# The low part of every second down-projection weight unit, made by a negated cast and an adding DMA

## The chip, the cores and the metric

The kernel runs on one NeuronCore of one Trainium2 chip. The core has a matmul engine (TensorE, in the profile PE for the matmuls and PEld for the weight loads that overlap them), three engines for elementwise work (VectorE or DVE, ScalarE or ACT, GpSimd or POOL) and SyncE (SP), which here only issues DMAs. Each engine works through its own queue in order and waits for others by semaphores. Sixteen DMA engines move data between HBM and SBUF, the on-chip memory of 128 partitions; matmuls write to PSUM. DMAs can be issued from the queues of SP, ACT and POOL.

The metric is the device time of the program in microseconds (us), as the median of several runs. The profile is one further execution, recorded instruction by instruction.

## The reference

The reference is a two-layer decoder trunk on 256 tokens of width 2048, in float32. Layer 0 mixes with gated linear attention, layer 1 with a causal attention that has forget gates; both attend to 256 memory tokens as well. What bears on this change is the channel mixer, which each layer ends with:

```python
def conv_ffn(h, w_up, conv_w, conv_b, w_down):
    u = causal_dwconv(h @ w_up, conv_w, conv_b)
    a, val = split_cols(u, [FFN_HIDDEN, FFN_HIDDEN])
    return (jax.nn.silu(a) * val) @ w_down
```

`FFN_HIDDEN` is 5632, so the down projection multiplies a 256 x 5632 activation by a 5632 x 2048 weight and adds the product to the residual stream, `x = x + conv_ffn(h, ...)`, once for each of the two layers.

## The kernel before

**Two parts for each number.** TensorE multiplies numbers in a shortened float32 (type `fp32r` in the profile). To keep accuracy, weights and activations are each held as a high part, which is the value rounded to that type, and a low part, the value minus its high part. A product is then three matmuls: high by high, high activation by low weight, low activation by high weight. Activations sit in SBUF with both parts (`bufA` and `bufB`, tiles A and B in the profile). Weights come from HBM once, in full float32, and are split on the way.

**Weight units.** The host lays all weights out as one array `wp`, cut into units of mostly 128 x 1024 float32 (512 KB). For the down projections a unit holds two blocks of 128 hidden channels by 512 output columns. The function `load_unit` (lines 185 to 200) takes a unit in: SP issues the DMA into a tile `raw` (line 196, four buffers), and ACT casts `raw` to the high part `whi` (line 199, three buffers). `split_unit` (line 202) calls it and then has DVE subtract, `wlo = raw - whi` (line 208, three buffers). Both `whi` and `wlo` go through their three buffers in turn, so the cast of a unit can start only when the matmuls of the unit three places before it have ended.

**The two kinds of projection.** `proj_fm` (used for the up projections; matmuls at lines 233, 234 and 236) has channels on the output's partitions. `proj_tm` (line 246; matmuls at lines 270, 271 and 272) has tokens there; the down projections go through it. For one unit it issues 12 matmuls: two halves of the tokens, two channel blocks, three products. Line 270 is high by high, line 271 uses the low part of the weight, line 272 the high part again with the low part of the activation. The weights are the moving operand, so each of the 12 streams 512 columns.

**Stages.** `ffn` (line 780) cuts the 5632 hidden channels into three parts of 16, 16 and 12 blocks of 128 (`PARTS`). For each part it runs the up projections of that part, which leave the activations in A or B, and then four down projections of 512 output columns each, added to the residual stream by DVE at line 774. So a down stage has 4 x 8, 4 x 8 or 4 x 6 units, a layer has 88 and the kernel 176. In the last projection of layer 1 a pool named `spare` holds units 3 to 5, and the second half of the tokens runs four units behind the first.

**What sets the order.** The program is written as one sequence; a scheduler orders each engine's queue by priorities and by its own estimates of time. Loading and splitting of a unit stand in a block of raised priority (`AHEAD`, 300 places ahead), so casts and subtractions are put as early as their buffers allow. In the order that results, the matmuls of a down unit begin with two of line 270, one for each half of the tokens, before the first of line 271.

Of the kernel before, what the change touches and what calls it, by code (L numbers as in the profile page):

```python
# [13 lines left out]
F32R = mybir.dt.float32r  # L14
I32 = mybir.dt.int32
AF = mybir.ActivationFunctionType
ALU = mybir.AluOpType
PSUM = bass.MemoryType.PSUM

P = 128  # L20
# [17 lines left out]
NUNIT = 1024  # L38
AHEAD = 300
# [99 lines left out]
def _trunk(ctx: ExitStack, tc: tile.TileContext, xt, xtok, memt, wp, wgu, gns, gfin, cnv, par, msk, out):  # L139
    nc = tc.nc  # L140
    where, _ = _layout()
    V, S, TE = nc.vector, nc.scalar, nc.tensor

    const = ctx.enter_context(tc.tile_pool(name="const", bufs=1))
    wpool = ctx.enter_context(tc.tile_pool(name="wpool", bufs=4))
# [39 lines left out]
    def load_unit(unit, pieces=1, before=None, pool=wpool, whole=False):  # L185
        off, kcs, n = unit
        w = len(kcs) * n
        raw = wpool.tile([P, NUNIT], F32, name="raw", tag="raw", bufs=4)
        hi = pool.tile([P, NUNIT], F32R, name="whi", tag="whi", bufs=3)
        src = wp[off : off + P * w].rearrange("(p n) -> p n", p=P)  # L190
        for i in range(pieces):
            if before is not None:
                before(i)
            s = slice(i * w // pieces, (i + 1) * w // pieces)
            if not whole:
                loads.append(nc.sync.dma_start(raw[:, s], src[:, s]))
            elif i == 0:
                loads.append(nc.sync.dma_start(raw[:, :w], src))
            casts.append(S.activation(hi[:, s], raw[:, s], AF.Copy))  # L199
        return raw, hi, w  # L200

    def split_unit(unit, pieces=1, before=None, pool=wpool, whole=False):
        with tc.high_priority(offset=AHEAD):
            raw, hi, w = load_unit(unit, pieces, before, pool, whole)
            lo = pool.tile([P, NUNIT], F32R, name="wlo", tag="wlo", bufs=3)
            for i in range(pieces):
                s = slice(i * w // pieces, (i + 1) * w // pieces)
                V.tensor_tensor(lo[:, s], raw[:, s], hi[:, s].bitcast(F32), ALU.subtract)  # L208
        return hi, lo

    def proj_fm(key, src, evac, before=None):

        units = where[key]
        total = sum(len(u[1]) for u in units)
        acc = [pacc.tile([P, 512], F32, name="acc", tag="acc") for _ in range(2)]
        base = min(min(u[1]) for u in units)
        done = 0
        for n, unit in enumerate(units):
            if before is None:
                hi, lo = split_unit(unit)  # L220
            else:
                hi, lo = split_unit(unit, 2, lambda half: before(n, half), whole=n > 0)
            for j, kc in enumerate(unit[1]):
                for c in range(2):
                    product(acc[c], c, total - 1, done, src[kc - base], hi, lo, j)
                done += 1
        for c in range(2):
            evac(c, acc[c])
# [17 lines left out]
    def proj_tm(key, src, evac, spare=None):  # L246

        units = where[key]  # L250
        n = units[0][2]
        base = min(min(u[1]) for u in units)
        acc = [pacc.tile([P, 512], F32, name="acc", tag="acc") for _ in range(2)]
        ahead = 0 if spare is None else 4
        ready = {}
        for i in range(len(units) + ahead):
            for b, u in ((0, i), (1, i - ahead)):
                if not 0 <= u < len(units):
                    continue
                if b == 0:  # L260
                    ready[u] = split_unit(units[u], pool=wpool if spare is None or u < 3 else spare)
                hi, lo = ready[u]
                kcs = units[u][1]
                a = acc[b][:, :n]
                xs = slice(b * P, (b + 1) * P)
                for j, kc in enumerate(kcs):
                    s = slice(j * n, (j + 1) * n)
                    xk = src[kc - base]
                    last = u == len(units) - 1 and j == len(kcs) - 1
                    TE.matmul(a, xk[:, 0, xs], hi[:, s], start=u == 0 and j == 0, stop=False)  # L270
                    TE.matmul(a, xk[:, 0, xs], lo[:, s], start=False, stop=False)  # L271
                    TE.matmul(a, xk[:, 1, xs], hi[:, s], start=False, stop=last)  # L272
                if u == len(units) - 1:
                    evac(b, a)
# [138 lines left out]
    with tc.tile_pool(name="load", bufs=1) as lp:  # L413
# [55 lines left out]
        with tc.issue_after(loads[-1].ins):  # L469
            for i in range(KC):  # L470
                nc.sync.dma_start(xf[i], xt[i])
            nc.sync.dma_start(part, par)
            nc.sync.dma_start(mask[:, M_FOX:], msk[:, M_FOX:])
        proj_tm(("mv", 0), bufA, mv_out(0))
        for i in range(KC):
            split(bufB, i, xf[i], gain("mix0", i))
        for j in range(2):
            proj_fm(("mk", 1, j), bufA, mk_out(1, j))
            if j == 0:
# [3 lines left out]
                for f in range(4):  # L483
                    for b in range(2):
                        nx.add(f, b)
        proj_tm(("mv", 1), bufA, mv_out(1))


    def gla(nx):
        h, mix = bufB, bufA  # L490
        with tc.tile_pool(name="gla", bufs=1) as gp:
# [14 lines left out]
            def first_values(b, a):  # L506
                S.activation(v0[:, b, :], a[:, :DV], AF.Copy, scale=nx.col()[:, b : b + 1])
                take(b, a[:, DV:])
                if b:
                    S.activation(glr, turn(), AF.Copy)  # L510

            proj_tm(("gv", 0), h, first_values)

            def take_mq(j):
# [297 lines left out]
    def preparing(name, dst, also=None):  # L812
        n = StreamNorm()

        def then(f, b):
            n.add(f, b)
            if b == 0:
                return
            for i in range(4 * f, 4 * f + 4, 2):
                ps = work("s", 2)  # L820
                for j in range(2):
                    for c in range(2):
                        o = j * T + c * P
                        k = (i + j) % 4 * P
                        TE.transpose(ps[:, o : o + P], x[f][:, c, k : k + P], ident)  # L825
                for j in range(2):
                    split(dst, i + j, ps[:, j * T : (j + 1) * T], gain(name, i + j))
                if also is not None:
                    also(i, ps)

        return n, then

    gla(nx)
    n, then = preparing("ffn0", bufB)
# [14 lines left out]
    n, then = preparing("ffn1", bufA)  # L849
# [104 lines left out]
```

## Time and profile before

| what | value |
|---|---|
| median of the runs | 2302.16 us (2302.14 to 2302.43, 3 runs) |
| span of the profiled execution, first to last instruction | 2300.7 us |
| PE busy | 2286.8 us |
| PEld busy | 1977.8 us |
| DVE busy | 1614.6 us |
| ACT busy | 1252.9 us |
| POOL busy | 3.0 us |
| read from HBM | 425.87 MB |

The profiled execution's own time is taken as its span of 2300.7 us; the 1.5 us by which the median of the unprofiled runs stands above it lie before the first and behind the last instruction.

How to read the rows: the page begins with the busy time of each engine, then a strip of 40 equal time slices, then the DMA queues, the chain of work that ended last, the costliest groups of instructions and the DMA issues. A group's row names its line, engine and operation, `out<-in` with the program's tile names, the shape, how often it ran (`x`), its busy time, the mean duration of one in ns, and then the idle time of that engine directly before these instructions with what ended it. A view of waits lists who waited for whom. A timeline lists single instructions with their start in us from the beginning of the span, their duration, and in brackets the idle time before them. Matmuls are pipelined: each is listed with 0.39 us from its start to its modelled end, while the next starts 0.23 us after it, so a busy PE is not a count of work. "us to landing" is the time from the issue of a DMA until its data are known to have arrived.

### The profile page before, as it was taken

What the parts mean: (1) busy time and instruction counts of PE and PEld (TensorE: products, weight loads), DVE (VectorE), ACT (ScalarE), POOL (GpSimd) and SP (SyncE); (2) the same over time, 40 slices, a digit from 0 to 9 for tenths busy, and PEclk for the clock granted to TensorE, in tenths of its full rate; (3) what the DMA queues carried; (4) which work ended last, traced back from release to release, by engine and by line L of the source; (5) the groups of instructions that cost most, each with busy time, mean ns of one, the idle gap of its engine ahead of it and who ended that gap; (6) DMA issues with size and microseconds to landing.
All of it is one profiled execution on the core that took longest, in us unless ns stands there. A gap on an engine that the chain in (4) does not pass through costs nothing.

```text
span 2300.7 us, 33144 instructions
## 1 busy us (share of the span) xinstructions
PE 2286.8 (99%) x12392; PEld 1977.8 (86%) x12392; DVE 1614.6 (70%) x2639; ACT 1252.9 (54%) x1961; POOL 3.0 (0%) x19
## 2 busy tenths in 40 slices
PE   9999999999999999999999999999999999999998
PEld 7889888888888888888888998888888888888886
DVE  7568987577765777557767557657776577756775
ACT  7555565555553555445565555556554455534554
POOL 0000000000000000000000000000000000000000
PEclk9999999999999999999999999999999999999999
DMA  8644455555555555555555564555555555555554
GB/s 317 196 160 160 150 165 177 187 182 190 190 190 194 187 191 189 192 191 189 190 183 185 180 194 158 166 191 188 186 191 192 192 187 189 190 195 191 186 190 156
DMA packets 124745, 430.15 MB, mean 187 GB/s; under 512 B 14108, under 2 KB 18600, under 8 KB 124456
## 3 DMA queue, kind: packets, MB, share of 16 engines
q1 hardware_dynamic: 124152, 427.24, 55.7%
q8 instruction: 97, 1.59, 0.3%
q10 hardware_dynamic: 432, 0.79, 0.1%
q14 instruction: 64, 0.52, 0.1%
HBM read 425.87 MB, written 2.11 MB: 186 GB/s over the span
## 4 chain that ended last, share of the span: by engine, by line
PE 99%; DMA 0%; ACT 0%; DVE 0%; issue 0%; SPq 0%; DVEq 0%; ACTq 0%
PE acc L233 37%; PE acc L234 20%; PE acc L271 12%; PE acc L272 12%; PE acc L270 12%; PE acc L236 2%; PE ps_s L825 0%; PE ps_s L614 0%; PE ps_t L388 0%; PE ps_s L395 0%; PE ps_o L406 0%; DMA mt<-memt 0%; PE ps_s L739 0%; PE ps_o L633 0%; PE ps_o L755 0%; PE ps_s L533 0%
## 5 line engine op out<-in xcount | busy, mean ns | idle before, releaser
L208 DVE TENSOR_TENSOR wlo<-raw,whi 128x1024 fp32r<-128x1024 f32 (+4 forms) x812 | 972.7, 1199 | 547.3 <-ACT whi L199 533.3
L199 ACT ACTIVATE whi<-raw 128x1024 fp32r<-128x1024 f32 (+4 forms) x812 | 843.5, 1040 | 775.7 <-PE acc L272 370.6
L233 PE MATMUL acc<-B,whi 128*128 128x512 f32 x1980 | 684.1, 396 | 0.0
L233 PE MATMUL acc<-A,whi 128*128 128x512 f32 x1680 | 579.1, 396 | 1.9 <-DVE A L300 1.5
L234 PE MATMUL acc<-B,wlo 128*128 128x256 f32 x2112 | 551.2, 281 | 0.0
L234 PE MATMUL acc<-A,wlo 128*128 128x256 f32 x1792 | 463.9, 281 | 0.7 <-DVE wlo L208 0.7
L233 PEld LDWEIGHTS acc<-B,whi 128*128 128x128 f32 x1980 | 360.9, 188 | 69.0
L234 PEld LDWEIGHTS acc<-B,wlo 128*128 128x128 f32 x2112 | 397.7, 188 | 21.7
L234 PEld LDWEIGHTS acc<-A,wlo 128*128 128x128 f32 x1792 | 337.3, 188 | 21.6 <-DVE wlo L208 1.7
L233 PEld LDWEIGHTS acc<-A,whi 128*128 128x128 f32 x1680 | 304.9, 188 | 58.8 <-DVE A L300 1.9
L271 PE MATMUL acc<-wlo,B 128*128 128x512 f32 (+3 forms) x736 | 274.9, 374 | 1.2 <-DVE wlo L208 1.2
L272 PE MATMUL acc<-whi,B 128*128 128x512 f32 (+3 forms) x736 | 274.0, 373 | 0.0
L270 PE MATMUL acc<-whi,B 128*128 128x512 f32 (+3 forms) x736 | 247.6, 372 | 0.0
L271 PE MATMUL acc<-wlo,A 128*128 128x512 f32 x544 | 212.6, 391 | 0.0
L272 PE MATMUL acc<-whi,A 128*128 128x512 f32 x544 | 211.8, 389 | 0.0
L270 PE MATMUL acc<-whi,A 128*128 128x512 f32 x544 | 192.6, 391 | 0.0
L241 ACT ACTIVATE part<-acc 128x256 f32<-128x256 f32 x240 | 90.0, 375 | 163.1 <-PE acc L236 163.1
L271 PEld LDWEIGHTS acc<-wlo,B 128*128 128x128 f32 x736 | 138.2, 188 | 21.0 <-DVE wlo L208 1.6
L272 PEld LDWEIGHTS acc<-whi,B 128*128 128x128 f32 x736 | 138.3, 188 | 18.7
L270 PEld LDWEIGHTS acc<-whi,B 128*128 128x128 f32 x736 | 137.5, 188 | 18.7
L243 DVE TENSOR_TENSOR wholes<-acc,part 128x256 f32<-128x256 f32 x240 | 101.1, 421 | 66.3 <-ACT part L241 65.9
L272 PEld LDWEIGHTS acc<-whi,A 128*128 128x128 f32 x544 | 102.2, 188 | 21.2
(201 smaller groups left out, 1571.2 us busy)
## 6 DMA issues: line engine op xcount, KB each, us to landing
raw<-wp SPq DMA_DIRECT2D x743, 512.0 KB, 3.5
raw<-wp SPq DMA_DIRECT2D x32, 384.0 KB, 3.1
raw<-wp SPq DMA_DIRECT2D x24, 388.0 KB, 3.5
raw<-wp SPq DMA_DIRECT2D x8, 400.0 KB, 3.0
xf<-xt SPq DMA_DIRECT2D x16, 128.0 KB, 4.5
x<-xtok SPq DMA_DIRECT2D x4, 512.0 KB, 6.7
mt<-memt SPq DMA_DIRECT2D x3, 512.0 KB, 7.1
cb<-cdram SPq DMA_DIRECT2D x12, 128.0 KB, 3.3
```

Of the source, the lines that this page charges most:

```text
L199: casts.append(S.activation(hi[:, s], raw[:, s], AF.Copy))
L208: V.tensor_tensor(lo[:, s], raw[:, s], hi[:, s].bitcast(F32), ALU.subtract)
L233: TE.matmul(a, hi[:, s], both, start=done == 0, stop=False)
L234: TE.matmul(a[:, :T], lo[:, s], both[:, 0, :], start=False, stop=False)
L236: TE.matmul(a, hi[:, s], both, start=False, stop=True)
L241: S.activation(t, a[:, T:], AF.Copy)
L243: V.tensor_tensor(r, a[:, :T], t, ALU.add)
L270: TE.matmul(a, xk[:, 0, xs], hi[:, s], start=u == 0 and j == 0, stop=False)
L271: TE.matmul(a, xk[:, 0, xs], lo[:, s], start=False, stop=False)
L272: TE.matmul(a, xk[:, 1, xs], hi[:, s], start=False, stop=last)
```

## The change

A second way to make the low part is added, `rest_by_dma`, and `proj_tm` takes it in the down projections for units with an odd number. It loads and casts the unit as before. Then ACT writes the negated high part into `wlo`: it casts `raw` with a scale of -1, which rounds the same way. A DMA issued from POOL's queue then reads the same 512 KB of `wp` from HBM a second time and adds them to what lies in `wlo`, so that `wlo = w - high(w)`. DVE has no part in these units. Even units, and all other projections, are made as before. The number of buffers is unchanged.

```diff
+    def rest_by_dma(unit, pool):
+        off, kcs, n = unit
+        w = len(kcs) * n
+        with tc.high_priority(offset=AHEAD):
+            raw, hi, w = load_unit(unit, 1, None, pool)
+            lo = pool.tile([P, NUNIT], F32R, name="wlo", tag="wlo", bufs=3)
+            S.activation(lo[:, :w], raw[:, :w], AF.Copy, scale=-1.0)
+            nc.gpsimd.dma_start(lo[:, :w], wp[off : off + P * w].rearrange("(p n) -> p n", p=P), accum_op=ALU.add)
+        return hi, lo
+
     def split_unit(unit, pieces=1, before=None, pool=wpool, whole=False):
...
                 if b == 0:
-                    ready[u] = split_unit(units[u], pool=wpool if spare is None or u < 3 else spare)
+                    take = rest_by_dma if key[0] == "down" and u % 2 else split_unit
+                    ready[u] = take(units[u], pool=wpool if spare is None or u < 3 else spare)
                 hi, lo = ready[u]
```

Each down projection has 4, 4 or 3 odd units, so 44 in a layer and 88 in the kernel take the new way. In the order of the changed kernel, ACT's queue has the negated cast of an odd unit directly ahead of its plain cast nearly throughout, POOL's queue has the 88 DMAs, and the matmuls of each unit keep their two leading ones of the line that is 270 before.

## The prediction

> **What bounds the kernel now.** I read the page's table of engines and its chain first, then the waits of PE, and last the timeline and the DMA rows of a down stage.
>
> ```profile
> span 2300.7 us, 33144 instructions
> PE 2286.8 (99%) x12392; PEld 1977.8 (86%) x12392; DVE 1614.6 (70%) x2639; ACT 1252.9 (54%) x1961; POOL 3.0 (0%) x19
> ...
> PE 99%; DMA 0%; ACT 0%; DVE 0%; issue 0%; SPq 0%; DVEq 0%; ACTq 0%
> ```
>
> PE is busy for all but 13.9 us (2300.7 less 2286.8), and the chain that ended last runs through PE alone. Another engine matters only where it makes PE wait, and it hardly ever does. The waits of PE (total us, times, longest) are:
>
> ```profile
> PE acc L233 <- DVE A L300: 1.5, 1, 1.5
> PE ps_o L176 <- DVE B L173: 1.4, 1, 1.4
> PE acc L271 <- DVE wlo L208: 1.2, 1, 1.2
> PE acc L234 <- DVE wlo L208: 0.7, 1, 0.7
> ```
>
> A low part kept PE's matmuls waiting twice in the whole kernel, for 1.9 us. So the question is how long before its use a low part can be started, and how much of that time the new way takes. The timeline of a down stage answers the first half:
>
> ```profile
> 702.10 0.62 PE L270 MATMUL acc<-whi,A 128*128 128x512 f32 x2
> 702.30 1.06 ACT L199 ACTIVATE whi<-raw 128x1024 fp32r<-128x1024 f32 x1 [1.66 <-PE acc L272]
> ...
> 703.40 1.23 DVE L208 TENSOR_TENSOR wlo<-raw,whi 128x1024 fp32r<-128x1024 f32 x1 [0.30 <-ACT whi L199]
> ...
> 704.82 0.62 PE L270 MATMUL acc<-whi,A 128*128 128x512 f32 x2
> 705.02 1.06 ACT L199 ACTIVATE whi<-raw 128x1024 fp32r<-128x1024 f32 x1 [1.66 <-PE acc L272]
> ...
> 707.54 0.62 PE L270 MATMUL acc<-whi,A 128*128 128x512 f32 x2
> 707.77 0.19 PEld L271 LDWEIGHTS acc<-wlo,A 128*128 128x128 f32 x1
> ```
>
> A unit takes PE 2.72 us (starts at 702.10, 704.82, 707.54). The cast at 702.30 waited for PE, for the unit that had just ended and gave up its buffers. With three buffers, the cast belongs to the unit that starts at 707.54, behind those of 702.10 and 704.82. Its low part is ready at 704.63; the first instruction to use it would start at 707.77. From the start of the cast there are 5.47 us, of which cast and subtraction take 2.33. The slack is 3.1 us in every unit, and it is set by the buffers: nothing can begin earlier.
>
> How busy the DMA engines are there, and how long a load takes, the rows of the same stage (670 to 740 us) say. The columns of the first are the stretch, its length, the busy time and instructions of PE, PEld, DVE, ACT and POOL, the granted clock, the DMA share and GB/s:
>
> ```profile
> 670.00:740.00 70.00, 70.00 (x311) 57.96 (x310) 35.46 (x32) 27.30 (x26) 0.00 (x0) 1.00 0.60 195
> L208 DVE TENSOR_TENSOR wlo<-raw,whi x26: 1224/1226/1227, 670.8 to 738.8; 128x1024 fp32r<-128x1024 f32 x26
> L199 ACT ACTIVATE whi<-raw x26: 1061/1061/1062, 669.7 to 737.7; 128x1024 fp32r<-128x1024 f32 x26
> q1 hardware_dynamic: 3738, 13.62, 59.4%
> DMA to landing us min/median/max: 4.2/4.3/5.1
> ```
>
> One load of 512 KB for each 2.72 us keeps the queue at 59.4%, so it costs all 16 engines 1.62 us (0.594 x 2.72), and it lands 4.3 us after its issue: 1.62 of moving and 2.7 of fixed time.
>
> **The change part by part.**
>
> *DVE loses 88 subtractions*, 88 x 1.226 = 108 us of its busy time. In this stage DVE is busy 35.46 of 70 us and PE waits for nothing, so this saves nothing on the path. What it could save elsewhere is the last rival.
>
> *ACT gains 88 casts*, taken at the price of the plain one: 88 x 1.061 = 93 us. ACT is busy 27.30 of 70 us here and the rest covers them. The negated cast mostly stands ahead of the plain one of its unit. The plain one is then done at 702.30 + 2.12 = 704.42 and wanted at 707.54, so a cover of 3.1 us hides the 1.06; without it each odd unit would pay 1.06, 93 us in all. Behind the pair in ACT's queue stands the cast of the next even unit, which can't start before 705.02.
>
> *SP's loads.* The raw buffer of an odd unit is given up by ACT at 704.42 in place of DVE at 704.63, no later than now. So the loads are issued as before, and with four raw buffers each is issued some two units before its cast. Nothing on the path, as long as DMA time is left.
>
> *The DMA that adds* is the step that counts. On POOL's queue it waits for the negated cast of its own unit, and behind it stand only the DMAs of later odd units and a few memsets that PE does not want soon. It cannot start before 703.36 (702.30 + 1.06) and must have landed at 707.77, so it has 4.4 us. No row shows a DMA issued from POOL, or one that adds. Bounds from the nearest rows:
>
> ```profile
> raw<-wp SPq DMA_DIRECT2D x743, 512.0 KB, 3.5
> x<-xtok SPq DMA_DIRECT2D x4, 512.0 KB, 6.7
> mt<-memt SPq DMA_DIRECT2D x3, 512.0 KB, 7.1
> ```
>
> The least is a plain load of the same size, 3.5 us as the median of the kernel and 4.3 in this stage: both fit into 4.4, and then the edit costs nothing. As upper bound I take the plain one with everything against it. An addition reads two sources, the weights and what lies in `wlo`, so its moving part may double: 1.62 more. One or two loads share the engines with it: 1.62 or 3.24 more. That is 4.3 + 1.62 + 3.24 = 9.2 us. Loads that compete with others do land that late already: 6.7 and 7.1 us for 512 KB.
>
> Between these I take 4.3 + 1.62 + 1.62 = 7.5 us: a second source, and one competing load, since one is issued every 2.72 us and the time is more than that. [...] So the low part lands at 703.36 + 7.5 = 710.9, and PE waits 3.1 us from 707.77.
>
> On the price of the second source: by the rows the moving costs between 1.62 us (a source in SBUF that costs nothing) and 3.24. [...]
>
> *The sum.* Does each of the 88 odd units pay 3.1 us? No. The next odd unit's buffer is given up by the even unit that ends before the wait begins, so its DMA starts on time and gains the wait as lead: it has 5.47 + 3.1 us. It is not late, and the one after it is late again. So 44 waits, 44 x 3.1 = 136 us. On the profiled execution's 2300.7 us this gives 2437, and with the 1.5 us by which the median of the runs (2302.16) stands above the span, 2438 us.
>
> The DMA engines allow it: a pair of units would use 2 x 1.62 + 3.24 = 6.5 us of them and takes 2 x 2.72 + 1.55 = 7.0. But they could not carry it at the old pace of 5.44 us for a pair: if latency were no matter, the doubled moving alone would cost 88 x 1.04 = 92 us.
>
> **The rivals.**
>
> *The DMA is hidden* (no change). For it: a plain load lands in 4.3 us where 4.4 are to be had. Against it: 0.1 us of slack, with a second source and a second load on the same engines. Time 2302 us. [...]
>
> *The addition moves at the price of a copy.* 4.3 + 1.62 = 5.9 us with one competing load, a wait of 1.5 us, 44 x 1.5 = 66 us: 2368 us.
>
> *The adding DMA is dearer than two copies*, in its descriptors or its moving. With three times the moving (3.24 more) and two competing loads (3.24) it takes 10.8 us, the wait is 6.4, 44 x 6.4 = 282 us: 2584 us. For it: no row of an adding DMA bounds its price. Against it: 512 KB in competition with other loads landed after a median of 7.1 us at most.
>
> *The waits bring the clock down.* PE's granted clock is 1.00 in the stage, and PE has no gap there, so the rows do not tell what gaps do. If each of the 44 waits were followed by one unit at half the clock, that would be 44 x 2.72 = 120 us on top of the forecast: 2558 us. [...]
>
> *Faster.* The freed 108 us of DVE end the waits that PE has for DVE. Its place are the four rows above, its price all of them, 1.5 + 1.4 + 1.2 + 0.7 = 4.8 us: 2297.4 us. It decides only if the adding DMAs are hidden and nearly all of these waits end, one of which stands at the kernel's first matmuls (L173) and one at an activation's low part (L300), where nothing is changed.
>
> **How the numbers follow.** Forecast (2438) 0.42, copy price (2368) 0.25, hidden (2302) 0.10, dearer (2584) 0.15, clock (2558) 0.05, faster (2297) 0.03. Within 0.2% (4.6 us) is about what a measurement of this kernel cannot tell from no change. Faster 0.03, same 0.10, slower 0.87. The range leaves out hidden and faster (0.13) and the end of the dearer case beyond its own price (0.07 of it): from 2335, half of the copy case's 66 us, to 2590.
>
> **What the profile will show.** If I am right: PE idles about 136 us more, all of it in the six down stages; a row of PE or PEld at the low-part matmul that waits for the adding DMA, about 44 times with about 3 us each; that DMA's landing near 7.5 us; DVE busy near 1507, ACT near 1346; DMA share in the down stage from 0.60 to about 0.9; HBM read larger by 46 MB (88 x 524,288 bytes). Wrong would be: landings under 4.4 us (hidden), waits at every odd unit (then the buffers are not what starts the next DMA), late loads of `raw` (then the DMA engines are full), or a granted clock below 1.00.

## The result and the profile after

The changed kernel takes 2480.69 us (median of 4 runs, 2475.2 to 2487.41) against 2302.15 us before: a ratio of 1.0776, 95% interval [1.0756, 1.0797], 178.5 us slower. The forecast was 2438 us with a range from 2335 to 2590.

From the page of the changed kernel, the span, the busy times, the two large DMA queues (packets, MB, the time of their packets as a share of the time of 16 engines) and the two large kinds of DMA issue (the last number is the median time to landing). The changed file's lines from 202 on stand 10 or 11 higher: line 282 is the low-part matmul that was 271, line 208 the negated cast, line 209 the adding DMA. In the runs further down the numbers shift again by a few lines; the tile names tell the rows apart.

```profile
span 2482.4 us, 33431 instructions
PE 2342.3 (94%) x12392; PEld 2000.1 (81%) x12392; DVE 1511.9 (61%) x2551; ACT 1335.1 (54%) x2049; POOL 79.0 (3%) x107
...
q1 hardware_dynamic: 124152, 427.24, 50.7%
q0 software_dynamic: 12672, 46.14, 10.8%
...
raw<-wp SPq DMA_DIRECT2D x743, 512.0 KB, 3.5
wlo<-wp POOLq DMA_DIRECT2D x88, 512.0 KB, 7.5
```

Queue q0 is POOL's. By the time of its packets one adding DMA takes 0.108 x 2482.4 / 88 = 3.05 us of all 16 engines; a plain load of the same 512 KB takes 0.507 x 2482.4 x 0.524 / 427.24 = 1.54 us. The waits of PE have a new first row, and the granted clock is lower than the 0.999 of before:

```profile
PE acc L282 <- DMA wlo<-wp: 124.1, 57, 4.7
PE ps_o L176 <- DVE B L173: 1.5, 1, 1.5
PE acc L243 <- DVE A L311: 1.2, 1, 1.2
```

```profile
core 0: 2482.4 us, clock 0.982
```

How one wait comes about shows in the timeline of a down stage (dots stand for rows left out, those of the weight loads among them):

```profile
700.23 1.06 ACT L208 ACTIVATE wlo<-raw 128x1024 fp32r<-128x1024 f32 x1 [1.39 <-PE acc L282]
...
701.58 0.86 POOL L209 DMA_DIRECT2D wlo<-wp  x1 [6.63 <-ACT wlo L208]
...
705.81 1.06 ACT L208 ACTIVATE wlo<-raw 128x1024 fp32r<-128x1024 f32 x1 [1.38 <-PE acc L282]
705.84 0.61 PE L281 MATMUL acc<-whi,A 128*128 128x512 f32 x2
...
707.16 0.86 POOL L209 DMA_DIRECT2D wlo<-wp  x1 [4.72 <-ACT wlo L208]
...
708.30 0.50 PE L282 MATMUL acc<-wlo,A 128*128 128x512 f32 x1 [1.85 <-DMA wlo<-wp]
...
713.42 1.07 PE L281 MATMUL acc<-whi,A 128*128 128x512 f32 x4
...
714.33 0.39 PE L282 MATMUL acc<-wlo,A 128*128 128x512 f32 x1
...
718.86 0.61 PE L281 MATMUL acc<-whi,A 128*128 128x512 f32 x2
...
721.56 0.64 PE L282 MATMUL acc<-wlo,A 128*128 128x512 f32 x1 [2.09 <-DMA wlo<-wp]
...
722.00 0.63 PE L283 MATMUL acc<-whi,A 128*128 128x512 f32 x1
...
722.43 0.63 PE L281 MATMUL acc<-whi,A 128*128 128x512 f32 x1
```

Three odd units start here, at 705.84, 713.42 and 718.86. The first waits 1.85 us for the DMA that POOL took up at 701.58. The DMA of the second was taken up at 707.16, during that wait, and is in time. The third is late again, by 2.09 us. Behind this last wait the matmuls follow each other every 0.43 us and are listed with 0.63, where 0.23 and 0.39 are usual: they run at half the clock (the granted clock from 721.80 to 725.10 is 0.50).

**Where the 181.7 us of span went.** PE's idle time rose from 13.9 to 140.1 us (2482.4 less 2342.3), by 126.2, nearly all of it the row of 124.1. PE's busy time rose by 55.5 us (2342.3 less 2286.8) for the same instructions. The lower clock accounts for (0.999 - 0.982) x 2482.4 = 42 us of that. Another 15 us are waits that are drawn as busy: at a wait, the matmul before it is drawn to its modelled end, 0.16 us past the usual next start, and the one behind it has its successor 0.34 us later instead of 0.23, together 0.27 us at each of 57 waits. So the waits cost 124 + 15 = 139 us and the clock about 42.

### The profile page after: what moved, and what is told of

Same layout as the page of the kernel before. It is cut to its first block, busy times and chain, and to the rows that moved or that the text cites. A ratio compares the mean times of both kernels' runs of the same rounds, so it can differ in the third digit from the quotient of the medians.

```text
span 2482.4 us, 33431 instructions
## 1 busy us (share of the span) xinstructions
PE 2342.3 (94%) x12392; PEld 2000.1 (81%) x12392; DVE 1511.9 (61%) x2551; ACT 1335.1 (54%) x2049; POOL 79.0 (3%) x107
## 3 DMA queue, kind: packets, MB, share of 16 engines
q1 hardware_dynamic: 124152, 427.24, 50.7%
## 5 line engine op out<-in xcount | busy, mean ns | idle before, releaser
L218 DVE TENSOR_TENSOR wlo<-raw,whi 128x1024 fp32r<-128x1024 f32 (+4 forms) x724 | 864.9, 1196 | 718.6 <-ACT whi L199 706.2
L282 PE MATMUL acc<-wlo,B 128*128 128x512 f32 (+3 forms) x736 | 286.6, 390 | 69.0 <-DMA wlo<-wp 67.9
L283 PE MATMUL acc<-whi,B 128*128 128x512 f32 (+3 forms) x736 | 281.7, 383 | 0.0
L282 PE MATMUL acc<-wlo,A 128*128 128x512 f32 x544 | 224.6, 413 | 56.2 <-DMA wlo<-wp 56.2
L281 PE MATMUL acc<-whi,B 128*128 128x512 f32 (+3 forms) x736 | 251.3, 379 | 0.0
L283 PE MATMUL acc<-whi,A 128*128 128x512 f32 x544 | 220.5, 405 | 0.0
L281 PE MATMUL acc<-whi,A 128*128 128x512 f32 x544 | 195.6, 400 | 0.0
L282 PEld LDWEIGHTS acc<-wlo,A 128*128 128x128 f32 x544 | 106.5, 196 | 90.6 <-DMA wlo<-wp 68.3
L283 PEld LDWEIGHTS acc<-whi,B 128*128 128x128 f32 x736 | 142.8, 194 | 19.3
L281 PEld LDWEIGHTS acc<-whi,B 128*128 128x128 f32 x736 | 141.0, 192 | 20.6
```

## The experiments

The theory was that a single delay, the way from the freed buffer to the landed sum, is longer than the lead that three buffers give; that half of the adding DMA's moving is its second source; and that the waits lower the clock. The rivals were the way through POOL's queue, DMA engines that are full, and the work added to ACT. The ratios below are to the kernel before.

### The second source

```diff
-            nc.gpsimd.dma_start(lo[:, :w], wp[...].rearrange("(p n) -> p n", p=P), accum_op=ALU.add)
+            nc.gpsimd.dma_start(lo[:, :w], wp[...].rearrange("(p n) -> p n", p=P))
```

> The DMA of the odd units overwrites wlo with the weights instead of adding to it; the low part of those units is then the whole weight, so this leaves out the subtraction. Theory (the second source doubles the moving, 1.5 us, on top of a long way through POOL's queue): landing falls from 7.5 us to about 6, waits of PE from 124 us to about 80, few gaps long enough to lower the clock, time about 2390 us. Rival 1 (the way through POOL's queue is what is slow): landing stays above 7 us and the time above 2460 us. Rival 2 (only the addition is slow): landing about 4.4 us, no waits, 2302 us.

Measured: 2395.66 us, ratio 1.0409 [1.0392, 1.0427]. Queue, DMA issue and wait of PE on it:

```profile
q0 software_dynamic: 12672, 46.14, 6.8%
wlo<-wp POOLq DMA_DIRECT2D x88, 512.0 KB, 6.1
```

```profile
PE acc L282 <- DMA wlo<-wp: 62.8, 52, 3.8
```

A copy by the same way takes 0.068 x 2390.2 / 88 = 1.85 us of the engines instead of 3.05, lands 1.4 us earlier, and halves the waits; POOL itself is busy with it for 0.53 us instead of 0.86. So making it an addition is worth 85 of the 178 us. The other 93 us are a copy's own way, which POOL's queue takes without any addition: both rivals fall. That the price of the addition is its second source is the reading of the prediction; the run shows the price alone.

### The casts alone

```diff
-            nc.gpsimd.dma_start(lo[:, :w], wp[...].rearrange("(p n) -> p n", p=P), accum_op=ALU.add)
```

> The negated cast of the odd units stays and the adding DMA is left out (so the low part of those units is the negated high part, and the second read of the weights is left out). Theory: the cast costs nothing on the path and the 88 subtractions that DVE loses save nothing: 2302 us within 0.2%. Rival (ACT's second cast holds up casts behind it, or DVE's relief is worth something): up to 93 us more, or 2297 us.

Measured: 2302.21 us, ratio 1.0 [0.999, 1.001]. The 88 casts on ACT are hidden, and the 88 subtractions that DVE no longer makes are worth nothing. All of the loss comes with the DMA.

### Half as many

```diff
-                    take = rest_by_dma if key[0] == "down" and u % 2 else split_unit
+                    take = rest_by_dma if key[0] == "down" and u % 4 == 1 else split_unit
```

> Only every fourth unit (1, 5, ...) goes the new way, 44 or so in place of 88. Theory (each wait is the latency of one DMA against the lead, and a wait gives lead to the next odd unit only): now every one of them waits, about 2.4 us each, 105 us, plus some 40 us for the clock: about 2450 us, so half of the DMAs cost nearly as much as all of them. Rival 1 (the cost is in proportion to the adding DMAs): half of 178 us, 2391 us. Rival 2 (full DMA engines): four units need 4 x 1.54 + 3.04 = 9.2 us of 10.9, so 2302 us.

Measured: 2448.77 us, ratio 1.0642 [1.0626, 1.0658]. The number of such units is 48 (units 1 and 5 of eight or six).

```profile
PE acc L282 <- DMA wlo<-wp: 102.4, 43, 3.8
```

With 55% of the DMAs, 82% of the loss is left (146.5 of 178.5 us). In the changed kernel 57 of 88 wait, here 43 of 48. A wait gives the next DMA its lead only where that DMA is already on its way during the wait; four units apart none is. Of the five that do not wait, four stand in the stages of six units, where the unit two places ahead is made the new way too and waits. Cost in proportion to the DMAs (2391 us) and full engines (2302 us) both fall.

### More lead for the low parts

The odd low parts get three buffers of their own, in a pool of the channel mixer (`own.append(fp if spare is None else spare)` in `ffn`):

```diff
-            lo = pool.tile([P, NUNIT], F32R, name="wlo", tag="wlo", bufs=3)
+            lo = own[-1].tile([P, NUNIT], F32R, name="wlo", tag="wlo", bufs=3)
```

> The low parts of odd units get three buffers of their own, so the negated cast and the adding DMA of an odd unit may start some units earlier; all work stays. Theory (the lead given by three buffers is what is too short): the waits of PE vanish, the clock is back at 1.00, time 2302 to 2315 us although the same DMAs land no earlier. Rival (the 16 DMA engines are full: a pair of units needs 2 x 1.54 + 3.04 = 6.1 us of them and PE takes 5.44): at least 88 x 0.68 = 60 us stay, 2362 us or more, with PE waiting for casts of late loads.

Measured: 2400.01 us, ratio 1.0426 [1.041, 1.0441]. That is neither: 81 us of the loss went, 98 stayed. The rows that say what is late now are a wait of the negated casts for loads, which the changed kernel does not have, beside what is left of PE's waits:

```profile
ACT wlo L210 <- DMA raw<-wp: 249.2, 77, 7.6
```

```profile
PE acc L284 <- DMA wlo<-wp: 41.7, 58, 1.9
PE acc L284 <- DVE wlo L220: 11.8, 36, 0.9
PE acc L283 <- ACT whi L199: 4.4, 3, 3.6
```

Two causes fit: engines that are nearly full and so land the loads late, or loads that are asked for too late. Four runs were to part them.

### Full engines, or late loads

First, own buffers with the copying DMA, which needs less engine time (the two edits above together):

> Own buffers for the odd low parts as before, and the DMA overwrites in place of adding (this leaves out the subtraction in the odd units). What is left of the cost with own buffers, 98 us, is either (i) DMA engines that are nearly full, or (ii) ACT's queue, where a negated cast that waits for a late load holds up plain casts. By (i) a pair of units now needs 2 x 1.54 + 1.84 = 4.9 us of the engines where PE takes 5.44: time 2302 to 2320 us. By (ii) the loads are as late as before: 2370 us or more.

Measured: 2320.98 us, ratio 1.008 [1.0063, 1.0097], almost what (i) asked for and far from the 2370 us or more of (ii). Then own buffers with every fourth unit:

> Own buffers, the adding DMA only in every fourth unit (48 in place of 88). Four units need 4 x 1.54 + 3.06 = 9.2 us of the engines where PE takes 10.9. If lead and engine time are all that counts, nothing is left: 2302 to 2310 us. If each adding DMA has a cost of its own that lead does not hide, 48/88 of 98 us, 53 us, are left: 2355 us.

Measured: 2335.86 us, ratio 1.0147 [1.0132, 1.0162]. Full engines would have left nothing here, so this speaks against (i), and neither of the two expectations holds: less stayed than a cost for each DMA would leave. Third, own buffers and three more buffers for the loads of odd units, all DMAs and additions in place:

```diff
-        raw = wpool.tile([P, NUNIT], F32, name="raw", tag="raw", bufs=4)
+        if rawpool is None:
+            raw = wpool.tile([P, NUNIT], F32, name="raw", tag="raw", bufs=4)
+        else:
+            raw = rawpool.tile([P, NUNIT], F32R, name="whi", tag="whi", bufs=3).bitcast(F32)
...
-            raw, hi, w = load_unit(unit, 1, None, pool)
+            raw, hi, w = load_unit(unit, 1, None, pool, rawpool=own[-1])
```

> Own buffers for the odd low parts, and three further buffers for the loads of the odd units (seven in all in place of four), so loads are issued earlier. By (i), full DMA engines: at least 60 us stay, 2362 us or more. By (ii), late loads in front of ACT's queue: most of the 98 us go, 2305 to 2335 us.

Measured: 2311.92 us, ratio 1.0043 [1.0028, 1.0058], inside the range of (ii). The same stretch of a down stage in the changed kernel, in the one with own low parts, and in this one (columns as in the prediction: busy PE, PEld, DVE, ACT, POOL, clock, DMA share, GB/s), and this one's adding DMA:

```profile
670.00:740.00 70.00, 60.74 (x247) 48.06 (x246) 15.40 (x16) 31.88 (x32) 8.63 (x10) 0.95 0.84 221
670.00:740.00 70.00, 61.31 (x251) 45.58 (x249) 16.39 (x16) 30.10 (x30) 8.63 (x10) 1.00 0.88 240
```

```profile
670.00:740.00 70.00, 70.00 (x309) 57.68 (x308) 18.60 (x18) 36.55 (x38) 10.35 (x12) 1.00 1.01 278
wlo<-wp POOLq DMA_DIRECT2D x88, 512.0 KB, 7.3
```

The engines move 278 GB/s where the other two move 221 and 240, the adding DMA still takes 7.3 us to land, and PE has no gap in these 70 us. So (i) is out, and with it my reading of the share as a capacity: packets of two queues overlap in it, and it stands at 1.01 here. What was left came from loads that are asked for too late: three more buffers for them take 88 of the 98 us away. How it works is read from the rows, not shown by a run of its own: with the negated cast ahead in ACT's in-order queue, a cast that waits for its load (249.2 us in all with own low parts alone) holds the casts behind it, and these give the raw buffers back. The copy's good result (2321 us) speaks against (ii) as it was written, which had the loads as late as before. They were not: from 670 to 740 us they landed after a median of 5.7 us with the copy, 8.3 with the addition. So earlier requests and shorter landings both help. Fourth, the load buffers alone, with the low parts in their three buffers:

> Three further buffers for the loads of the odd units, but the low parts keep their three buffers: the fourth corner beside the changed kernel (neither), own low-part buffers (2400 us) and both (2312 us). Theory (the lead is set by the buffers of the low part, and loads matter only once that lead is longer): nothing gained, 2470 to 2490 us. Rival (late loads are a cost of their own): about 2480 - 88 = 2392 us.

Measured: 2474.1 us, ratio 1.0745 [1.0729, 1.0761].

```profile
PE acc L287 <- DMA wlo<-wp: 122.9, 59, 4.5
```

The four corners are 2481 (neither), 2474 (loads), 2400 (low parts), 2312 (both). The lead of the low part comes first; loads matter only behind it. No run beats the kernel before.

### Filling the gaps

```diff
+                    if b == 0 and j == 0 and key[0] == "down" and u % 2:
+                        idle = work("o")
+                        for i in range(7):
+                            TE.matmul(idle, xk[:, 0, xs], hi[:, s], start=i == 0, stop=i == 6)
```

> Seven matmuls whose result nobody reads are put into each odd down unit ahead of its first matmul with the low part; all else as changed. They are 88 x 7 x 0.227 = 140 us of PE time. Theory (the gaps cost 124 us of waiting and, through the lowered clock, some 55 us more): the added matmuls fill the gaps, the clock stays at 1.00, and the kernel gets faster by adding work: about 2302 + 140 + 5 to 15 = 2450 us. Rival (the clock is not lowered by the gaps, or costs nothing): 2480 us or more.

Measured: 2496.11 us, ratio 1.0843 [1.0827, 1.0859].

```profile
PE 2441.9 (98%) x13008; PEld 2094.1 (84%) x13008; DVE 1512.8 (61%) x2551; ACT 1337.2 (54%) x2049; POOL 79.1 (3%) x107
```

```profile
core 0: 2492.8 us, clock 0.997
```

```profile
PE acc L286 <- DMA wlo<-wp: 35.5, 26, 3.2
```

With three matmuls in place of seven:

> As the kernel with seven unread matmuls in each odd down unit, but with three: 88 x 3 x 0.227 = 60 us of PE time. [...] Rival (the rise of PE's busy time is not the clock): the kernel takes as long as the changed one or longer, 2480 us or more.

Measured: 2485.54 us, ratio 1.0795 [1.0775, 1.0815], with clock 0.989, 86.4 us of waits and 2390.1 us of busy PE. The forecast of a faster kernel, 2450 us with seven, failed, and the rivals' times (2480 us or more) came, but not their reason, a clock that gaps do not lower. What did come is the clock: 0.982, 0.989, 0.997 with no, three and seven filling matmuls. PE's busy time beyond before and beyond the fills (616 or 264 times 0.227 us, which is 140 or 60) falls with it: 55.5, 43.4 and 15.3 us. The clock alone, as 0.999 less the granted one, times the span (2482.4, 2489.1 and 2492.8 us), gives 42, 25 and 5 us. But waits and fills together grew, 124, 146 and 175 us: a fill is paid in full in the odd units that would not have waited (31 of 88 in the changed kernel; three or seven fills in each are 21 or 49 us, about the growth of 22 and 51). So it is shown that filled gaps keep the clock up; that the changed kernel would be 42 us faster at full clock is accounting, not a measurement.

## Why the prediction was right, and where it was off

The direction and the range held, and the 43 us between the forecast of 2438 and the measured 2481 are nearly one term, the clock.

- *The slack.* Read from the cast at 702.30 as set by the buffers. Right: own buffers for the low part, followed by buffers for the loads, take 169 of the 178.5 us away while the DMA still needs 7.3 us.
- *The DMA that adds: 7.5 us.* Measured 7.5 as the median of the kernel, from 5.2 to 9.6; in the first down stage, from whose rows the terms were read, the median is 6.8, in the others 6.9 to 8.3, so the exact agreement is partly luck. Of its parts, the moving was rightly doubled: 3.05 us of the engines against 1.54 for a load, though only 1.65 times the 1.85 of the copy by the same queue. That the second source is what doubles it no run shows, and that one competing load makes up the third part was not tested. What I left out is 0.29 us from the end of the negated cast (706.87) to POOL's taking up of the DMA (707.16).
- *The sum: 44 waits of 3.1 us, 136 us.* Measured 139 us, of which 124.1 stand in the row of waits, but as 57 waits with a mean of 2.2 us in it. Landings scatter, so some neighbours both wait; and the first odd unit of each of the six stages is 4.1 to 4.7 us late. The total came out right and its two factors did not, which is luck.
- *"The DMA engines ... could not carry it at the old pace."* Wrong, though it entered no sum: with more buffers they carried it at almost the old pace. I had added up packet time as if queues never overlapped.
- *Edits costed at nothing.* Casts and subtractions: 2302.21 us with both and without the DMA. DVE was to be near 1507 and is 1511.9, ACT near 1346 and is 1335.1, the DMA share 0.9 and is 0.84 from 670 to 740 us.
- *The rivals.* Hidden fell, and faster with it. Copy price, forecast at 2368 us, is refuted by q0's 3.05 us, and the copy itself took 2395.66. Dearer did not come. The clock, given 0.05 and 120 us if one whole unit followed each of 44 waits at half speed, was the one that came, on top of the forecast as it was built. It was mis-sized: that each wait is followed by a whole unit at half speed no run shows; 22 of the 57 waits brought the clock down, to 0.50 for 85 us in all, which makes the 42 us. The sum had it at nothing; that is the failed term, and a granted clock below 1.00 was among the prediction's own signs of being wrong.

## What to carry to other kernels

Where an engine is busy for 99% of the time, price a change by the longest single way from a freed buffer to the first use, against the lead that the buffers give: here 8.9 us (1.06 + 0.29 + 7.5) against 5.47. Moving work to idle engines or queues then needs buffers along the whole way, and one more set of them at one place only uncovers the next (2481, 2400, 2312 us). Waits of a few us on TensorE cost more than their length here, about 42 us beyond the 139, because 22 of the 57 brought the granted clock down to 0.50; a DMA share of 0.84 or 0.88 was no proof of full engines, which moved more (278 GB/s in place of 221 or 240) once the buffers let them.

## What the runs showed of the hardware that was not expected

**Not every wait lowered the clock.** In the profile of the changed kernel the granted clock falls to 0.50 in 22 places of the down stages, 85 us in all, each of them during a wait of PE for the adding DMA or within 1.5 us behind its end. The other 35 of the 57 waits have none. The 22 waits took 1.80 to 4.69 us and the 35 took 0.29 to 3.04, so the length of a wait alone did not decide it. Of the waits in the timeline above, that of 1.85 us left the clock at 1.00 (from 708.30 to 711.60 us), and that of 2.09 us was followed by 0.50.

**The adding DMA took the engines twice as long as a load here**: 3.05 us of all engines against 1.54 for a load of the same size, and 1.85 for a copy by the same queue. The shortest landing in the changed kernel was 5.2 us, the median 7.5.
